# Activations of the gate spread over the down projection, PSUM in two pools, early weight halves moved from GpSimd to VectorE

## The chip, the core and the metric

The kernel runs on one core of one Trainium2 chip. The metric is the device time of one execution in microseconds; the time before is the median of three runs. The engines of the core are called PE (TensorE, the matrix multiplications; PEld is its loading of stationary operands), DVE (VectorE), ACT (ScalarE), POOL (GpSimd) and SP (SyncE, which here issues most of the transfers).

## The reference, cut to what matters

One layer over 1024 tokens of 1024 channels: a mixer, then a router, then sixteen experts, each of which takes the 128 tokens that score highest for it. All is float32.

```python
def expert_choice_ffn(h, w_r, w1, w3, w2):
    bn, n, _ = h.shape
    cap = EC_FACTOR * n // N_EXPERTS                      # 128
    aff = jax.nn.softmax((h @ w_r).astype(jnp.float32), axis=-1)
    gate, idx = lax.top_k(jnp.swapaxes(aff, 1, 2), cap)
    bidx = jnp.arange(bn)[:, None, None]
    xe = h[bidx, idx]
    hid = jax.nn.silu(jnp.einsum('becd,edf->becf', xe, w1)) * jnp.einsum('becd,edf->becf', xe, w3)
    ye = jnp.einsum('becf,efd->becd', hid, w2) * gate[..., None].astype(h.dtype)
    return jnp.zeros_like(h).at[bidx, idx].add(ye)

def reference(...):
    ...
        x = x + g1x * yx
        hx2 = rmsnorm(x, norm2_g[l]) * (1.0 + sc2x) + sh2x
        x = x + g2x * expert_choice_ffn(hx2, w_router[l], w1[l], w3[l], w2[l])
    return rmsnorm(x, final_g)
```

`w1` and `w3` are 1024x2048 for each expert, `w2` is 2048x1024.

## The kernel before, in words

**Products.** A float32 product is made of three matmuls: each operand is split into a rounded `hi` and the rest `lo`, and hi·hi, hi·lo and lo·hi are summed in PSUM. The weights of an expert come in 24 **units** of 128x2048 float32 (1 MB): eight each of w1, w3 and w2. A unit is loaded by SP into one of twelve buffers (`raw`), ACT copies it to `hi` (L104), and another engine subtracts, `lo = raw - hi` (L105). `presplit(n, engine)` does that for all units up to number n. `unit(key)`, called when PE comes to a unit, first splits ahead, up to two units past this one, always with DVE; the pool of the halves (`sp`) has three buffers, so a copy waits until PE has finished the unit three before.

**Experts.** The program is written in the order in which each engine shall work; nothing reorders it. One pass of the loop over e does: `up("3", e)` (eight units, matmuls L1251, L1253 and L1255 into four PSUM banks; in the first unit all three for two banks, then for the other two), with the gathered rows of the next expert transposed in between; `hidden(e)`, four multiplications on DVE, silu times the second product (L1270); `up("1", e+1)`, with the transposes of the hidden rows of e in between; `silu(e+1)`, four activations on ACT (L1264), one per bank; and `down(e)`, eight units (L1292, L1295, L1298) into two banks, then the evacuation (L1305) and a scatter-add by POOL. The pass e = 14 leaves out its `down`, so that `up("3", 15)` follows `silu(15)` directly; `down(14)` and `down(15)` come at the end.

**PSUM.** All results in PSUM come out of one pool of eight banks, taken in turn.

**Before the experts.** The router's scores of the last tile of tokens give, on DVE, sorted lists: MAX and MATCH_REPLACE steps, and compare steps L1017 and L1018, queued in `fills` and called one by one between other work by `fill(n)`. `router_sm(7)` is the softmax of the last tile (row sum L986 ... product `tv` L992). The end of the sort is the threshold T (L1176). From it come each token's place (`pos`, L1198), the one-hot matrix of an expert (`oh`, L1212, `route_oh`), its list of rows (`route`: `ix` L1223, `gate` L1224, the gather of rows `xe` by POOL L1229), and their transposes (L1239 to L1241), on which the first `up("1", 0)` waits. The halves of the first units are made along the way: unit 0, then 1, then 2, with POOL doing the subtraction; units 3 and 4, in a pool `sx` of their own, with DVE.

Of the kernel before, what the change touches and what calls it, by code (L numbers as in the profile page):

```python
# [20 lines left out]
P = 128  # L21
# [6 lines left out]
class Two:  # L28
    """a tensor in two tiles, halved along its second axis"""
# [16 lines left out]
def hybrid_layer(ctx, tc, x, c, ctxt, c_ctx, w_mod, b_mod, norm1_g, norm2_g, w_in, sgu_g, sgu_w,  # L46
# [13 lines left out]
    psp = ctx.enter_context(tc.tile_pool(name="ps", bufs=8, space=bass.MemoryType.PSUM))  # L60
# [6 lines left out]
    def bank(shape, name):  # L67
        return psp.tile(shape, F32, name=name, tag="bk")
# [8 lines left out]
    # ---- weights of the experts: loaded in units; each unit split into exact halves  # L77
# [41 lines left out]
    # ================================================================ phase 1  # L119
# [6 lines left out]
    # ---- loads of the first stage  # L126
# [10 lines left out]
    def wblk(n):  # L137
        """raw block n of 128 columns of w_in, loaded in pairs"""
        if n // 2 not in wraw:
            t = wb.tile([P, 8, 2 * P], F32, name="wraw")  # L140
            col = wcols[n // 2]
            nc.sync.dma_start(t, w_in[:, col:col + 2 * P].rearrange("(k p) f -> p k f", p=P))
            wraw[n // 2] = t
        return wraw[n // 2][:, :, (n % 2) * P:(n % 2 + 1) * P]
# [14 lines left out]
    # ---- constants  # L159
# [26 lines left out]
    # ---- parameter columns  # L186
# [6 lines left out]
    def rstd(dst, ssq, m, n, gap=lambda: None):  # L193
        """1 / sqrt(ssq / n + eps), refined by one Newton step; m is scratch"""
# [12 lines left out]
    # silu of the conditioning  # L207
# [12 lines left out]
    # ---- row normalisation: context in columns 8, 9 of stat  # L220
# [10 lines left out]
    def row_nr(o, n):  # L231
        """a Newton step for 1 / sqrt"""
# [9 lines left out]
    # 8 * log_sigmoid(lam), with log1p(z) = 2 atanh(z / (2 + z))  # L242
# [31 lines left out]
    # ---- modulation vectors: shift and scale of the first norm, as columns  # L274
# [54 lines left out]
    # ---- transposed, modulated inputs in exact halves  # L329
# [10 lines left out]
    def modsplit(srcs, k, s, hi, lo):  # L340
        """(src * scale + shift) of blocks k.. as hi + lo; a subtraction on DVE follows one step behind"""
# [17 lines left out]
    # ---- channel-major products with a block of 128 columns of w_in  # L359
# [8 lines left out]
    # ---- the other modulation vectors (gate 1, shift 2, scale 2, gate 2): rows summed on DVE, partitions on PE  # L368
# [37 lines left out]
    # ---- the first two blocks over all positions, transposes three steps ahead of the products  # L406
# [80 lines left out]
    # ---- recurrent branch: positions in the order (context, latent) forwards, (latent, context) backwards  # L487
# [110 lines left out]
    # ---- other channel-major blocks: u, then the gate of the recurrence  # L598
# [66 lines left out]
    # ---- gx (gelu, times the recurrence); meanwhile the remaining modulation vectors  # L665
# [7 lines left out]
    def split_wv(h, t):  # L673
        """(high, low) of the rows of block k"""
# [57 lines left out]
    # ---- v, token-major; gating of each chunk  # L732
# [65 lines left out]
    def scale_wo(h, ts):  # L798
        """gate 1 folded into the columns of w_out"""
# [62 lines left out]
    # ---- output projection, residual, second norm, router  # L862
# [24 lines left out]
    # scores by expert: one or two tiles in halves, each in 32 partitions  # L887
# [32 lines left out]
    def fill(n=1):  # L920
        """the next n steps of each queue; a number in the first queue waits for that many steps of the second"""
# [16 lines left out]
    # channels 256 q + 2 p + k of the second norm lie in the order (q k p)  # L938
# [64 lines left out]
    # ---- descending lists of the scores of each expert; the steps are queued and run between other work  # L1003
# [4 lines left out]
    def q_bitonic(n, v, dst, f=fills):  # L1008
        """v, n rows rising and then falling (or the reverse) -> descending"""
# [13 lines left out]
    def q_sort(i, dst, f=fills):  # L1023
        """the halves in WS[i] sorted and merged into dst, one row of CAP for each tile"""
# [14 lines left out]
    def q_fold(s, dst):  # L1039
        """rows 32.. joined to rows ..32: the CAP largest of each pair, descending"""  # L1040
# [64 lines left out]
    # the last tile, one half of the columns after the other  # L1105
# [32 lines left out]
    # by token and expert: the token, the score in exact halves, the token  # L1138
# [20 lines left out]
    presplit(1, G)  # L1159
# [8 lines left out]
    q_sort(5, L5)  # L1168
    while fills or fills2:
        fill()  # L1170
    presplit(2, G)
    # threshold: the 128th of the merged descending lists
# [4 lines left out]
    V.tensor_sub(tvr[:, :, :, 2], affs, tvr[:, :, :, 1])  # L1177
# [6 lines left out]
    # counts over the tiles before, four zero tiles in front  # L1184
# [14 lines left out]
    presplit(3, G)  # L1199
    pes.close()  # L1200

    # ================================================================ experts
# [13 lines left out]
    def route(e):  # L1216
        oh = OH.pop(e)
        p = bank([P, 4], "pr")
# [13 lines left out]
    def transpose_x(e):  # L1232
# [3 lines left out]
        for h in range(2):  # L1236
            p = bank([P, 4, P], "xp")
# [21 lines left out]

    def silu(e, pt):  # L1260
        sg[e] = []
        for b in range(4):
            s = mb.tile([P, 4, P], F32, name="sg", bufs=4)
            A.activation(s.rearrange("t j p -> t p j"), pt[b].rearrange("t (p j) -> t p j", j=4), AF.Silu)  # L1264
            sg[e].append(s)
# [6 lines left out]
    def transpose_h(e, bs):  # L1272
        for b in bs:
            p = bank([P, 4, P], "hp")
# [41 lines left out]
    while pieces:  # L1316
        load_next()
    presplit(4, V, sx)
    route_oh(1)
    presplit(5, V, sx)  # L1320
    g2row = mp.tile([P, D], F32, name="g2row")
# [7 lines left out]
    for e in range(NE):  # L1329
# [17 lines left out]
        if nxt:  # L1347
            hidden(e, up("3", e, mid))
            p1 = up("1", e + 1, {2: lambda: transpose_h(e, (0, 1)), 4: lambda: transpose_h(e, (2, 3))})
            silu(e + 1, p1)  # L1350
            if e + 2 < NE:
                down(e)
# [11 lines left out]
    # ================================================================ last expert's sum, final norm  # L1364
# [129 lines left out]
```

## Time and profile before

| | us |
|---|---|
| median of three runs | 1681.43 (1681.33 to 1681.81) |
| span of the profiled execution, first to last instruction | 1676.8 |
| of it PE / DVE / ACT / POOL busy | 1546.4 / 1394.0 / 1092.8 / 213.9 |

The span is 4.6 us less than the median, which holds what lies around the instructions too. The busy times are sums over the whole span: first the mixer and the router (to about 484 us), then the experts (to about 1660 us). The trace gives each instruction's start and length; several of one kind that follow closely stand in one row with their count (x4).

### The profile page before, as it was taken

The page shows a single profiled execution, that of the slowest core. Times are in us where ns is not written, and L with a number is a line of the kernel's source. Part 1 is how long each engine was busy: PE and PEld are TensorE (multiplying, and loading weights), DVE is VectorE, ACT ScalarE, POOL GpSimd, SP SyncE. Part 2 cuts the span into 40 slices and gives each one's busy share as a digit, 9 for nine tenths or more (in the row PEclk, how much of TensorE's full clock was granted, in tenths as well). Part 3 has the DMA queues.
Part 4 walks back from the last instruction along what each step waited for, and adds up shares of the span by engine and source line. Part 5 has one row for each costly group of instructions (what it writes and reads, how often), then busy time and mean ns, then how long its engine had stood idle before and what let it go on. Part 6 is the DMA issues. An engine that isn't in the chain of part 4 may idle for free.

```text
span 1676.8 us, 19242 instructions
## 1 busy us (share of the span) xinstructions
PE 1546.4 (92%) x7290; PEld 1262.6 (75%) x7290; DVE 1394.0 (83%) x1358; ACT 1092.8 (65%) x995; POOL 213.9 (13%) x160
## 2 busy tenths in 40 slices
PE   5899989889729999999999999999999999999995
PEld 2687779778627787877878787787877878788783
DVE  6669787867876898988989888898988989888897
ACT  6575746422326767777676777767777677777764
POOL 2411212532320000100101000010000101001002
PEclk8999999999859999999999999999999999999998
DMA  9010247333656999999999999999999999999855
GB/s 377 27 35 29 95 146 262 137 117 121 251 206 251 353 386 359 380 342 369 379 358 384 348 384 351 368 375 370 371 346 372 380 356 385 339 389 363 328 190 201
DMA packets 85932, 485.31 MB, mean 289 GB/s; under 512 B 11208, under 2 KB 20048, under 8 KB 35664
## 3 DMA queue, kind: packets, MB, share of 16 engines
q1 hardware_dynamic: 80912, 466.72, 72.8%
q0 software_dynamic: 4832, 17.33, 4.1%
q8 instruction: 57, 0.93, 0.2%
q14 instruction: 35, 0.29, 0.1%
q10 hardware_dynamic: 96, 0.03, 0.0%
HBM read 463.61 MB, written 20.45 MB: 289 GB/s over the span
## 4 chain that ended last, share of the span: by engine, by line
PE 68%; DVE 13%; ACT 10%; issue 4%; DMA 3%; POOL 2%; SPq 0%; ACTq 0%; DVEq 0%; POOLq 0%
PE h L1251 14%; PE h L1253 14%; PE h L1255 13%; PE ye L1295 6%; PE ye L1298 6%; PE ye L1292 5%; ACT sg L1264 3%; DVE lo L105 2%; ACT hi L104 2%; PE hp L1276 2%; DMA ring<-in_w_mod_dram 1%; PE pw L910 1%; PE pw L912 1%; PE xp L1239 1%; PE pw L914 1%
## 5 line engine op out<-in xcount | busy, mean ns | idle before, releaser
L105 DVE TENSOR_TENSOR lo<-raw,hi 128x2048 fp32r<-128x2048 f32 x381 | 863.3, 2290 | 154.1 <-ACT hi L104 152.8
L104 ACT ACTIVATE hi<-raw 128x2048 fp32r<-128x2048 f32 x384 | 733.3, 1919 | 260.7 <-PE h L1255 127.7
L1251 PE MATMUL h<-hi,xth 128*128 128x512 f32 x1024 | 288.6, 398 | 1.8 <-ACT hi L104 1.8
L1253 PE MATMUL h<-lo,xth 128*128 128x512 f32 x1024 | 282.2, 392 | 2.3 <-DVE lo L105 2.3
L1255 PE MATMUL h<-hi,xtl 128*128 128x512 f32 x1024 | 282.1, 392 | 0.0
L1253 PEld LDWEIGHTS h<-lo,xth 128*128 128x128 f32 x1024 | 192.6, 188 | 46.3 <-DVE lo L105 3.1
L1255 PEld LDWEIGHTS h<-hi,xtl 128*128 128x128 f32 x1024 | 192.5, 188 | 42.8
L1251 PEld LDWEIGHTS h<-hi,xth 128*128 128x128 f32 x1024 | 188.0, 189 | 40.4 <-ACT hi L104 2.7
L1295 PE MATMUL ye<-lo,hth 128*128 128x512 f32 x512 | 162.3, 398 | 18.5 <-DVE lo L105 18.5
L1292 PE MATMUL ye<-hi,hth 128*128 128x512 f32 x512 | 161.2, 396 | 0.0
L1298 PE MATMUL ye<-hi,htl 128*128 128x512 f32 x512 | 160.5, 394 | 0.0
L1308 POOL DMA_INDIRECT x2d<-ye,ix x15 | 50.1, 3340 | 815.4 <-DVE ye L1305 815.4
L1295 PEld LDWEIGHTS ye<-lo,hth 128*128 128x128 f32 x512 | 95.3, 188 | 46.2 <-DVE lo L105 24.6
L1298 PEld LDWEIGHTS ye<-hi,htl 128*128 128x128 f32 x512 | 96.3, 188 | 22.9
L1292 PEld LDWEIGHTS ye<-hi,hth 128*128 128x128 f32 x512 | 96.0, 188 | 22.3
L1264 ACT ACTIVATE sg<-h 128x512 f32<-128x512 f32 x64 | 62.9, 1146 | 2.2 <-PE h L1255 1.3
L1279 ACT ACTIVATE hth<-hp 128x512 fp32r<-128x512 f32 x64 | 35.0, 596 | 43.4 <-PE hp L1276 43.4
L388 DVE SCALAR_TENSOR_TENSOR ring<-ring,cs 128x1024 f32<-128x1024 f32 x28 | 46.0, 1642 | 11.9 <-DMA ring<-in_w_mod_dram 11.3
L362 PE MATMUL pu<-hxh,wh 128*128 128x512 f32 x128 | 50.9, 398 | 2.6 <-ACT g1row L721 2.6
L1229 POOL DMA_INDIRECT xe<-hx2d,ix x16 | 17.1, 1070 | 272.0 <-DVE gate L1224 241.2
L363 PE MATMUL pu<-hxh,wl 128*128 128x512 f32 x128 | 50.8, 397 | 0.0
L364 PE MATMUL pu<-hxl,wh 128*128 128x512 f32 x128 | 50.8, 397 | 0.0
(349 smaller groups left out, 1991.2 us busy)
## 6 DMA issues: line engine op xcount, KB each, us to landing
raw<-in_w_dram SPq DMA_DIRECT2D x383, 1024.0 KB, 7.3
ring<-in_w_mod_dram SPq DMA_DIRECT2D x32, 512.0 KB, 5.3
wmod<-in_w_mod_dram SPq DMA_DIRECT2D x8, 1024.0 KB, 9.6
wraw<-in_w_in_dram SPq DMA_DIRECT2D x6, 1024.0 KB, 7.1
xh<-in_x_dram SPq DMA_DIRECT2D x4, 1024.0 KB, 16.2
wor<-in_w_out_dram SPq DMA_DIRECT2D x4, 1024.0 KB, 8.4
xr<-in_x_dram SPq DMA_DIRECT2D x8, 512.0 KB, 4.3
x2d<-xr SPq DMA_DIRECT2D x8, 512.0 KB, 2.7
```

The source lines that it names most:

```text
L104: A.activation(hi, s, AF.Copy)
L105: eng.tensor_tensor(lo, s, hi, op=OP.subtract)
L362: PE.matmul(p, w[0][:, k], act[0][:, k], start=(k == 0), stop=False)
L363: PE.matmul(p, w[1][:, k], act[0][:, k], start=False, stop=False)
L364: PE.matmul(p, w[0][:, k], act[1][:, k], start=False, stop=(k == 7))
L1251: PE.matmul(pt[b], hi[:, k], wh[:, b * 512:(b + 1) * 512], start=(k == 0), stop=False)
L1253: PE.matmul(pt[b], hi[:, k], wl[:, b * 512:(b + 1) * 512], start=False, stop=False)
L1255: PE.matmul(pt[b], lo[:, k], wh[:, b * 512:(b + 1) * 512], start=False, stop=(k == 7))
L1264: A.activation(s.rearrange("t j p -> t p j"), pt[b].rearrange("t (p j) -> t p j", j=4), AF.Silu)
L1292: PE.matmul(pt[n], hi[:, j], wh[:, j2 * 1024 + n * 512:j2 * 1024 + n * 512 + 512], start=st_, stop=False)
L1295: PE.matmul(pt[n], hi[:, j], wl[:, j2 * 1024 + n * 512:j2 * 1024 + n * 512 + 512], start=False, stop=False)
L1298: PE.matmul(pt[n], lo[:, j], wh[:, j2 * 1024 + n * 512:j2 * 1024 + n * 512 + 512], start=False, stop=en)
```

## The change

Five things are different. The SILU of one bank gets a function of its own, and for e up to 13 the four are called after units 0, 2, 4 and 6 of `down(e)` instead of ahead of it. PSUM is one pool of eight banks until the experts begin; then it is a pool of six (h, ye, rb, fp) and one of two (pr, xp, hp), which wait tile by tile. The subtraction of unit 0 goes from POOL to DVE, at the same place of the program. Those of units 1 and 2 go from POOL to DVE, and from behind the sort and behind `pos` to behind `route(0)`; `route_oh(1)` is called ahead of units 3 and 4. A subtraction into `tvr` goes from behind T into the queue of sort steps. Comments are gone; lines after are higher by two or three.

```diff
@@ def hybrid_layer
-    psp = ctx.enter_context(tc.tile_pool(name="ps", bufs=8, space=bass.MemoryType.PSUM))
+    pss = ExitStack()
+    psp = pss.enter_context(tc.tile_pool(name="ps", bufs=8, space=bass.MemoryType.PSUM))
...
-    def bank(shape, name):
-        return psp.tile(shape, F32, name=name, tag="bk")
+    banks = [psp, psp]
+
+    def bank(shape, name, small=0):
+        return banks[small].tile(shape, F32, name=name, tag="bk")
@@ sort
-    presplit(1, G)
+    presplit(1, V)
     router_mm(7)
     fill(12)
     router_sm(7)
...
     q_sort(5, L5)
+    fills.insert(8, lambda: V.tensor_sub(tvr[:, :, :, 2], affs, tvr[:, :, :, 1]))
     while fills or fills2:
         fill()
-    presplit(2, G)
...
     V.tensor_reduce(T, m, axis=AX.X, op=OP.min)
-    V.tensor_sub(tvr[:, :, :, 2], affs, tvr[:, :, :, 1])
...
     V.scalar_tensor_tensor(pos, gt, FAR, eq, op0=OP.add, op1=OP.add)
-    presplit(3, G)
     pes.close()
@@ route, transpose_x, transpose_h
-        p = bank([P, 4], "pr")
+        p = bank([P, 4], "pr", 1)
...
-            p = bank([P, 4, P], "xp")
+            p = bank([P, 4, P], "xp", 1)
...
-            p = bank([P, 4, P], "hp")
+            p = bank([P, 4, P], "hp", 1)
@@ silu
+    def silu1(e, pt, b):
+        s = mb.tile([P, 4, P], F32, name="sg", bufs=4)
+        A.activation(s.rearrange("t j p -> t p j"), pt[b].rearrange("t (p j) -> t p j", j=4), AF.Silu)
+        sg.setdefault(e, []).append(s)
+
     def silu(e, pt):
-        sg[e] = []
         for b in range(4):
-            s = mb.tile([P, 4, P], F32, name="sg", bufs=4)
-            A.activation(s.rearrange("t j p -> t p j"), pt[b].rearrange("t (p j) -> t p j", j=4), AF.Silu)
-            sg[e].append(s)
+            silu1(e, pt, b)
@@ ahead of the experts, after route(0) and the loads
+    presplit(3, V)
+    route_oh(1)
     presplit(4, V, sx)
-    route_oh(1)
     presplit(5, V, sx)
+    pss.close()
+    for i, n in enumerate((6, 2)):
+        banks[i] = ctx.enter_context(tc.tile_pool(name=f"ps{n}", bufs=n, space=bass.MemoryType.PSUM,
+                                                  reuse_waits="tile"))
     g2row = mp.tile([P, D], F32, name="g2row")
@@ loop over e
             hidden(e, up("3", e, mid))
             p1 = up("1", e + 1, {2: lambda: transpose_h(e, (0, 1)), 4: lambda: transpose_h(e, (2, 3))})
-            silu(e + 1, p1)
             if e + 2 < NE:
-                down(e)
+                down(e, {u: lambda b=b: silu1(e + 1, p1, b) for b, u in enumerate((0, 2, 4, 6))})
+            else:
+                silu(e + 1, p1)
```

On ACT, from the middle of `up("1", 1)` to the transposes of the next expert in the middle of `up("3", 1)`, the program of before has these instructions in a row (`hth` are the transposed hidden rows, `sg` the SILU's output, `h_...` its bank):

```order
L1279 ACTIVATE hth<-hp 128x512 x2
L104 ACTIVATE hi<-raw 128x2048 x3
L1264 ACTIVATE sg<-h_4319 128x128x4
L1264 ACTIVATE sg<-h_4320 128x128x4
L1264 ACTIVATE sg<-h_4321 128x128x4
L1264 ACTIVATE sg<-h_4322 128x128x4
L104 ACTIVATE hi<-raw 128x2048 x11
L1240 ACTIVATE xth<-xp 128x512 x2
```

The changed program has at the same place:

```order
L1282 ACTIVATE hth<-hp 128x512 x2
L107 ACTIVATE hi<-raw 128x2048 x4
L1263 ACTIVATE sg<-h_4326 128x128x4
L107 ACTIVATE hi<-raw 128x2048 x2
L1263 ACTIVATE sg<-h_4327 128x128x4
L107 ACTIVATE hi<-raw 128x2048 x2
L1263 ACTIVATE sg<-h_4328 128x128x4
L107 ACTIVATE hi<-raw 128x2048 x2
L1263 ACTIVATE sg<-h_4329 128x128x4
L107 ACTIVATE hi<-raw 128x2048 x4
L1241 ACTIVATE xth<-xp 128x512 x2
```

The four activations stood together ahead of the copy for the third unit of `down`; now that copy stands ahead of the first of them, and two copies stand between any two.

On PE, at the first unit of a later `up("1", e+1)`, directly behind `up("3", e)`, the program of before has these matmuls, with the semaphores that each waits for (`h1_...` are the four banks, DVE_49 is the semaphore that DVE raises, at a value of each wait's own):

```order
L1251 MATMUL h1_5373<-hi_5322,xth_5256 128x512 [waits Activation_49]
L1251 MATMUL h1_5374<-hi_5322,xth_5256 128x512 [waits PE_49]
L1253 MATMUL h1_5373<-lo_5323,xth_5256 128x512 [waits DVE_49]
L1253 MATMUL h1_5374<-lo_5323,xth_5256 128x512
L1255 MATMUL h1_5373<-hi_5322,xtl_5257 128x512
L1255 MATMUL h1_5374<-hi_5322,xtl_5257 128x512
L1251 MATMUL h1_5375<-hi_5322,xth_5256 128x512 [waits PE_49]
L1251 MATMUL h1_5376<-hi_5322,xth_5256 128x512 [waits DVE_49,PE_49]
```

The changed program has:

```order
L1252 MATMUL h1_5380<-hi_5329,xth_5263 128x512 [waits Activation_49]
L1252 MATMUL h1_5381<-hi_5329,xth_5263 128x512
L1254 MATMUL h1_5380<-lo_5330,xth_5263 128x512 [waits DVE_49]
L1254 MATMUL h1_5381<-lo_5330,xth_5263 128x512
L1256 MATMUL h1_5380<-hi_5329,xtl_5264 128x512
L1256 MATMUL h1_5381<-hi_5329,xtl_5264 128x512
L1252 MATMUL h1_5382<-hi_5329,xth_5263 128x512 [waits DVE_49]
L1252 MATMUL h1_5383<-hi_5329,xth_5263 128x512 [waits DVE_49]
```

The third and fourth bank each have a wait for DVE of their own now. By the values of the semaphore and the addresses of the banks, they are the first two banks of `up("3", e)`, and the two waits are for the first and the second multiplication of `hidden(e)`; in the program of before no bank of `up("1", e+1)` was one of `up("3", e)`.

On DVE, at the end of the last tile's norm (`hx`), the program of before goes straight on with the steps of the sort:

```order
L1155 SCALAR_TENSOR_TENSOR hx_3494<-tm,ss_2519,SH2row 128x512 x2
L1017 TENSOR_TENSOR L_2542<-bt_3532 32x64
L1018 TENSOR_TENSOR L_2542<-bt_3532 32x64
L1049 TENSOR_TENSOR bt<-LS_2539,L_2542 32x128
L1028 MAX S_2522<-W_2520 64x8
```

The changed program has there:

```order
L1158 SCALAR_TENSOR_TENSOR hx_3494<-tm,ss_2519,SH2row 128x512 x2
L108 TENSOR_TENSOR lo<-raw,hi 128x2048
L1020 TENSOR_TENSOR L_2542<-bt_3532 32x64
L1021 TENSOR_TENSOR L_2542<-bt_3532 32x64
L1052 TENSOR_TENSOR bt<-LS_2539,L_2542 32x128
L1031 MAX S_2522<-W_2520 64x8
```

The subtraction of unit 0 stands ahead of the steps that `fill(12)` calls. The other two have joined the two that stood behind the first `gate` already, on both sides of `oh`:

```order
L1225 TENSOR_REDUCE gate<-pr 128x1
L108 TENSOR_TENSOR lo<-raw,hi 128x2048 x2
L1213 TENSOR_TENSOR oh<-iota_s,pos 128x1024
L108 TENSOR_TENSOR lo<-raw,hi 128x2048 x2
L1242 TENSOR_TENSOR xtl<-xp,xth 128x512 x2
```

So DVE does four of these subtractions, where it did two, between the first routing and the first transposes.

## Rows read from the trace of the kernel before

**Rows 1.** The page, part 4: the chain that ended last, by line.

```profile
PE h L1251 14%; PE h L1253 14%; PE h L1255 13%; PE ye L1295 6%; PE ye L1298 6%; PE ye L1292 5%; ACT sg L1264 3%; DVE lo L105 2%; ACT hi L104 2%; PE hp L1276 2%; DMA ring<-in_w_mod_dram 1%; PE pw L910 1%; PE pw L912 1%; PE xp L1239 1%; PE pw L914 1%
```

**Rows 2.** Windows: us; busy us per engine; granted clock; DMA share; GB/s.

```profile
643.40:1430.97 787.57, 773.00 (x3521) 632.07 (x3520) 689.88 (x430) 577.32 (x375) 47.86 (x22) 1.00 0.97 367
667.32:714.99 47.67, 47.67 (x226) 39.49 (x224) 44.57 (x32) 34.14 (x23) 4.35 (x2) 1.00 1.00 377
```

**Rows 3.** Timeline of the sort: start, length, engine, line, operation [idle before <-releaser].

```profile
448.19 0.22 DVE L992 TENSOR_SCALAR tv<-ex,ss 128x16 f32<-128x16 f32 x1
...
452.52 0.21 DVE L1017 TENSOR_TENSOR L<-bt 32x64 f32<-32x64 f32 x1
...
454.49 1.90 ACT L104 ACTIVATE hi<-raw 128x2048 fp32r<-128x2048 f32 x1
...
456.46 4.50 POOL L105 TENSOR_TENSOR lo<-raw,hi 128x2048 fp32r<-128x2048 f32 x1 [5.79 <-ACT hi L104]
...
457.43 0.17 DVE L986 TENSOR_REDUCE ss<-pl 128x1 f32<-128x16 f32 x1 [0.25 <-PE pl L982]
...
458.24 2.75 DVE L992 TENSOR_SCALAR tv<-ex,ss 128x16 f32<-128x16 f32 x1
...
464.68 9.01 POOL L105 TENSOR_TENSOR lo<-raw,hi 128x2048 fp32r<-128x2048 f32 x2 [3.72 <-ACT hi L104]
...
464.80 4.52 DVE L1018 TENSOR_TENSOR bt<-bt 32x64 f32<-32x64 f32 x1
...
469.44 4.33 DVE L1017 TENSOR_TENSOR bt<-bt 32x64 f32<-32x64 f32 x1
...
480.73 0.27 DVE L1176 TENSOR_REDUCE T<-bt 32x1 f32<-32x128 f32 x1
```

**Rows 4.** Timeline of DVE after the first routing.

```profile
487.81 2.28 DVE L105 TENSOR_TENSOR lo<-raw,hi 128x2048 fp32r<-128x2048 f32 x1
...
498.07 0.69 DVE L1241 TENSOR_TENSOR xtl<-xp,xth 128x512 fp32r<-128x512 f32 x1 [4.64 <-ACT xth L1240]
```

**Rows 5.** Waits: engine, line, releaser: us in total, times, longest us.

```profile
PE ye L1295 <- DVE lo L105: 18.5, 14, 1.3
```

**Rows 6.** Timeline of the down projection of expert 1.

```profile
642.91 3.93 ACT L1264 ACTIVATE sg<-h 128x512 f32<-128x512 f32 x4
...
646.63 5.51 ACT L104 ACTIVATE hi<-raw 128x2048 fp32r<-128x2048 f32 x3
...
648.59 6.70 DVE L105 TENSOR_TENSOR lo<-raw,hi 128x2048 fp32r<-128x2048 f32 x3 [3.48 <-ACT hi L104]
...
648.98 0.63 PE L1292 MATMUL ye<-hi,hth 128*128 128x512 f32 x2
...
650.94 0.30 PEld L1295 LDWEIGHTS ye<-lo,hth 128*128 128x128 f32 x2 [1.76 <-DVE lo L105]
...
653.37 0.64 PE L1292 MATMUL ye<-hi,hth 128*128 128x512 f32 x2
...
656.16 0.63 PE L1292 MATMUL ye<-hi,hth 128*128 128x512 f32 x2
...
656.36 1.92 ACT L104 ACTIVATE hi<-raw 128x2048 fp32r<-128x2048 f32 x1 [0.87 <-PE ye L1298]
...
658.31 2.29 DVE L105 TENSOR_TENSOR lo<-raw,hi 128x2048 fp32r<-128x2048 f32 x1 [0.50 <-ACT hi L104]
```

**Rows 7.** Timeline of the end of up("3", 1) and the start of up("1", 2).

```profile
620.52 2.47 DVE L1270 TENSOR_TENSOR sg<-sg,h 128x512 f32<-128x512 f32 x4
...
620.98 0.41 PEld L1251 LDWEIGHTS h<-hi,xth 128*128 128x128 f32 x2
```

**Rows 8.** The multiplications of L1270: lengths in ns, least, median, most.

```profile
L1270 DVE TENSOR_TENSOR sg<-sg,h x64: 673/678/681, 548.5 to 1602.4; 128x512 f32<-128x512 f32 x64
```

**Rows 9.** Timeline of the start of up("1", 15).

```profile
1550.27 0.42 PEld L1251 LDWEIGHTS h<-hi,xth 128*128 128x128 f32 x2
...
1550.74 2.47 DVE L1270 TENSOR_TENSOR sg<-sg,h 128x512 f32<-128x512 f32 x4
```

## The prediction

> **What bounds the kernel now.** I read the chain that ended last first. After the mixer it runs almost wholly through the experts' matmuls: L1251 to L1255 and L1292 to L1298 hold 58% of the span [rows 1]. Eleven experts, from the start of `down(1)` to that of `down(12)`, take 787.57 us, 71.60 each, with PE busy 98% of it at the full granted clock, 1.00 [rows 2]. So in the experts only what stops PE counts: 14.6 us of 787.57 are left, and the next view accounts for nearly all of them. The view of waits names the largest stop: 18.5 us in 14 pieces, in which the second step of a unit of `down` waits for `lo` from DVE [rows 5].
>
> The timeline of one `down` tells which unit and why [rows 6]. Four activations hold ACT from 642.91 to 646.84; only then come the copies that `down` needs next. The copy for the third unit ends at 648.55, its subtraction (2.29) at 650.88, and PE goes on at 650.94, 0.06 later. The third unit starts at 648.98, the fourth at 653.37, 4.39 apart; an undisturbed unit takes 656.16 − 653.37 = 2.79. So PE loses 1.60 per `down`. It is a wait of one place, and the rest of `down` is at PE's pace.
>
> Ahead of the experts the bound is DVE's sort. There I looked for operations that are longer than their kind: `tv` takes 2.75 where another tile's took 0.22, and two compare steps take 4.52 and 4.33 where the usual is 0.21 [rows 3]. Each lies under a subtraction of POOL, and ends with it: `tv` at 460.99 (POOL: 460.96), the two compares at 469.32 and 473.77, with POOL's two in one stretch of 9.01 from 464.68 to 473.69. DVE's compares stand still while POOL subtracts.
>
> **The change part by part.** The sum is made against the profiled span, 1676.8, and carried over to the median, 1681.43, with the 4.6 us around the span unchanged.
>
> *1. Subtractions off POOL during the sort.* Gone: 2.75 − 0.22, 4.52 − 0.21 and 4.33 − 0.21, together 10.96 us of DVE's chain to T at 480.73 [rows 3].
>
> *2. The subtraction of unit 0 on DVE.* It stands ahead of the steps of `fill(12)`, which began at 452.52. It waits for ACT's copy, which ends at 454.49 + 1.90 = 456.39, then takes 2.29 [rows 3, 6]: it ends near 458.7. Queued behind it are the sort steps that filled 452.52 to 457.18 (L986 starts at 457.43 after 0.25 idle): 4.66 us, now to 463.4, and L986, the softmax and the last list's sort behind them. L986 is 463.4 − 457.4 = 6.0 later. The moved `tvr` step costs about one step more, 0.3 at most. T comes at 480.73 − 10.96 + 6.0 + 0.3, 4.7 earlier. Bounds: 11.0 earlier if DVE's wait were free; nothing if the compares run slow for a reason other than POOL.
>
> *3. The subtractions of units 1 and 2 behind `gate`.* DVE has 2 × 2.28 = 4.6 us more between 487.81 and the first `xtl` at 498.07, and was idle 4.64 there, waiting for the transposes that follow the gather [rows 4]. The gather and the wait shift together with T. I price it at 0; without that cover it is 4.6.
>
> *4. SILUs in `down`.* The copy for unit u+2 now starts when unit u does, 0.20 after (656.16 to 656.36), and its subtraction ends at 658.31 + 2.29 = 660.60, 4.44 after the unit's start [rows 6]. It is wanted in the second step of unit u+2, at 2 × 2.79 + 0.46 = 6.04 (0.46 is two of a unit's twelve matmuls in 2.79): 1.6 us to spare. A SILU, (3.93/4 = 0.98 in the row of four, a little more by itself) comes behind a copy that ends 2.12 after the unit's start, so it ends near 3.2, when the next copy is due at 2.99. The delay of 0.2 is inside the 1.6. ACT has 8 × 1.92 + 4 × 1.1 = 19.8 us of work in 8 × 2.79 = 22.3. So the 1.60 goes whole: 14 experts (e = 0 to 13), 22.4 us. Nothing new is late: `up("3", e+1)` takes over the SILUs' banks, and the last SILU, called after unit 6, is done near 6 × 2.79 + 3.2 = 19.9, before the 22.3 at which it begins.
>
> *5. Six banks instead of eight.* The third and fourth bank of `up("1", e+1)` now wait for the first and second multiplication of `hidden(e)`. In the row of four multiplications of 2.47 us, each takes 0.68 [rows 7, 8], so they start 0.60 apart: the second ends at 620.52 + 0.60 + 0.68 = 621.80, and PE knows it at 621.86. The weight load for the fourth bank stood at 620.98 + 0.23 = 621.21 [rows 7], so it is held for 0.65. Not all of a hold is lost: in rows 6 loads were idle 1.76 and the unit lost 1.60, 0.16 less. That makes 0.49, and 14 × 0.49 = 6.9 us for e = 0 to 13. For e = 14 the multiplications start later against PE: the second ends at 1552.02, seen at 1552.08, and the load stood at 1550.27 + 0.23 = 1550.50 [rows 9], so 1.58 − 0.16 = 1.4. Together 8.3. Such a wait is not in the trace of before. Bounds: 0, if the banks come free in time after all; and 32.0, if the third bank waited for all four (620.52 + 2.47 + 0.06 = 623.05 against a load at 620.98, 2.07 each, and 1550.74 + 2.47 + 0.06 − 1550.27 = 3.0 for e = 14, none of it recovered). I take 8.3: the order shows a wait of its own for each bank. The pool of two I price at 0: its pairs of transposes lie two units apart, over 5 us, and an evacuation takes 0.69 on DVE [rows 4]; if PE waited for one per expert, it would be 16 × 0.69 = 11.
>
> **Sum.** −4.7 − 22.4 + 8.3 = −18.8: span 1658.0, median 1681.43 − 18.8 = **1662.6 us**.
>
> **The rivals.**
>
> *The bank wait costs nothing.* If the multiplications start a little earlier against PE or the hold is absorbed, −27.1: 1654.3. For it: the hold is only 0.65 long. Against it: PE is busy 98%, with no slack behind.
>
> *The front gives nothing.* DVE's early wait for the copy, or `xtl` coming late behind four subtractions (4.6 of 4.64 idle is a narrow cover), eats the 4.7: −14.1, 1667.3.
>
> *Memory takes over.* At 367 GB/s an expert moves 26.3 MB; if that were the limit, the period would stay 71.60 and only the front's 4.7 come: 1676.7. Against it: a stretch of 47.67 us moved 377 GB/s [rows 2], at which 26.3 MB take 69.7 us, under the forecast period of 71.60 − 1.60 + 0.49 = 70.5. The Trainium skill, "HBM Reference", Specifications, gives an effective 358 GB/s per core, and about 425 for a core that streams alone. By the 358, 26.3 MB would take 73.4 us, an estimate from that page; this trace's 367 is above it, and the core is alone.
>
> *The other side: the stall only moves.* If the copies come late behind the SILUs, four small stalls take the place of one: no gain in `down`, and the banks' 8.3 stays: −4.7 + 8.3 = +3.6, 1685.0. It decides when a SILU holds the next subtraction for 1.6 + 0.4 = 2.0 us, so that four stalls of 0.4 give back the 1.60. Against it: a SILU takes 1 us and falls mostly into ACT's idle time.
>
> *The other side: banks wait as a whole.* With the 32.0 of part 5, −27.1 + 32.0 = +4.9: 1686.3. It decides from 27.1 / 15 = 1.8 us per expert. For it only that one semaphore serves many waits; against it the two separate waits.
>
> **How the numbers follow.** Of a measurement of this kernel, 0.2% (3.4 us) is about what can be told from no change. Chances: the forecast 0.66 (its own range 1658 to 1666: the hold between 0.2 and 0.65 per expert, the front between 2 and 8), free banks 0.12, no front 0.12, memory 0.03, moved stall 0.04, whole banks 0.03. Memory at 1676.7 is still faster by 0.28%. So faster 0.66 + 0.12 + 0.12 + 0.03 = 0.93 less some for what I don't see, 0.92; the last two lie just over 0.2% slower, and I split their 0.07 and the rest as slower 0.04, same 0.04. The range takes in free banks at its lower end and the front's loss at its upper: 1654 to 1668.
>
> **What would show it right or wrong.** Right: no wait of L1295's successor for `lo` left, the third and fourth unit of `down` 2.79 apart, a new wait of PE at the first unit of `up("1")` for the multiplications, near 0.5 each in 14 places and 1.4 in one, no compare step on DVE over 1 us in the sort, the first `xtl` near 493.4, and 70.5 us per expert. Wrong: waits for `lo` spread over `down`, copies of ACT waiting for loads in most units, or compares that are slow without POOL. What would upset the sum most is a wait of PE in the experts that I counted as covered, since it comes 14 times.

## The result and the profile after

The changed kernel takes 1660.67 us (median of four runs, 1656.74 to 1663.98) against 1681.62 for the kernel before (1681.33 to 1682.18): a ratio of 0.988, with a 95% interval of 0.987 to 0.990. In a second set of runs the ratio was 0.9875 (0.985 to 0.990). The profiled execution has a span of 1658.4 us where 1658.0 was forecast; its own time is 1660.27.

In the rows of the changed kernel the copy and the subtraction are L107 and L108, the matmuls of `up` L1252, L1254 and L1256, those of `down` L1295, L1298 and L1301, the SILU L1263 and the multiplication L1273: not every line is higher by two or three than before.

The experts first. A window from the start of `down(1)` to that of `down(12)`, eleven experts (us; busy us by engine with counts; granted clock; DMA share; GB/s):

```profile
638.06:1413.80 775.74, 774.66 (x3522) 632.38 (x3521) 693.04 (x430) 577.29 (x374) 47.90 (x22) 1.00 0.98 373
```

That is 70.52 us per expert, where [rows 2] had 71.60, and PE is idle for 1.1 us of it all instead of 14.6 (most of the new hold, below, lies inside the modelled length of a matmul and does not show as idle time of PE). The view of waits has no row any more in which `down` waits for `lo`, which [rows 5] had 14 times; it has a new one, for weight loads of the first unit of `up("1")` behind the multiplications, and a small one for weight loads of `up("3")` behind SILUs (engine, line, releaser: us in total, times, longest):

```profile
PEld h L1252 <- DVE sg L1273: 11.9, 30, 1.2
PEld h L1252 <- ACT sg L1263: 2.7, 4, 0.8
```

The four of the second row lie in `up("3", 0)` and `up("3", 15)`, which follow their four SILUs directly and take over their banks. The prediction has no such wait, but it costs nothing: the kernel before waited at the same two places for the copies behind the SILUs, and the two ups took 26.11 and 25.11 us there and take 26.03 and 25.07 here.

```profile
PEld h L1251 <- ACT hi L104: 2.7, 2, 1.5
```

The first row counts thirty loads in fifteen places: the third and the fourth bank each wait. The timeline of one of the places:

```profile
613.72 0.42 PEld L1252 LDWEIGHTS h<-hi,xth 128*128 128x128 f32 x2
...
614.63 2.47 DVE L1273 TENSOR_TENSOR sg<-sg,h 128x512 f32<-128x512 f32 x4
...
615.36 0.19 PEld L1252 LDWEIGHTS h<-hi,xth 128*128 128x128 f32 x1 [0.31 <-DVE sg L1273]
615.36 1.10 PE L1252 MATMUL h<-hi,xth 128*128 128x512 f32 x2
615.96 0.19 PEld L1252 LDWEIGHTS h<-hi,xth 128*128 128x128 f32 x1 [0.41 <-DVE sg L1273]
```

The loads of the third and fourth bank go out at 615.36 and 615.96, 0.60 apart as the multiplications are; without a wait they would follow at about 615.09 and 615.31 (six matmuls after 613.72). The hold of the second is 0.65, as forecast; what it costs shows in the length of a pair of ups, on average 48.21 us where it was 47.66, so 0.55.

In `down(1)` the copies, SILUs and subtractions interleave, and the third unit (643.64) is followed by the fourth 2.79 later (646.43), where [rows 6] had 4.39:

```profile
640.08 1.10 ACT L1263 ACTIVATE sg<-h 128x512 f32<-128x512 f32 x1
...
641.05 1.92 ACT L107 ACTIVATE hi<-raw 128x2048 fp32r<-128x2048 f32 x1
...
643.00 2.29 DVE L108 TENSOR_TENSOR lo<-raw,hi 128x2048 fp32r<-128x2048 f32 x1 [0.50 <-ACT hi L107]
...
643.64 0.62 PE L1295 MATMUL ye<-hi,hth 128*128 128x512 f32 x2
...
646.43 0.62 PE L1295 MATMUL ye<-hi,hth 128*128 128x512 f32 x2
```

A copy starts 0.20 after its unit, as before; the SILU lies ahead of it in ACT's idle time. A `down` takes 22.31 us, before 23.93.

The sort, against [rows 3]: the subtraction of unit 0 waits 3.82 for ACT's copy, the row sum L989 starts at 463.12, `tv` takes 0.23, no compare step is long, and T comes at 475.86.

```profile
454.40 1.90 ACT L107 ACTIVATE hi<-raw 128x2048 fp32r<-128x2048 f32 x1
...
456.33 2.29 DVE L108 TENSOR_TENSOR lo<-raw,hi 128x2048 fp32r<-128x2048 f32 x1 [3.82 <-ACT hi L107]
...
463.12 0.15 DVE L989 TENSOR_REDUCE ss<-pl 128x1 f32<-128x16 f32 x1
...
463.91 0.23 DVE L995 TENSOR_SCALAR tv<-ex,ss 128x16 f32<-128x16 f32 x1
...
475.86 0.27 DVE L1179 TENSOR_REDUCE T<-bt 32x1 f32<-32x128 f32 x1
```

Behind `gate`, four subtractions stand where two stood [rows 4], and the first transposes' `xtl` is not held: its idle time, 4.64 before, is 0.35.

```profile
482.94 4.48 DVE L108 TENSOR_TENSOR lo<-raw,hi 128x2048 fp32r<-128x2048 f32 x2
...
488.47 4.49 DVE L108 TENSOR_TENSOR lo<-raw,hi 128x2048 fp32r<-128x2048 f32 x2
...
493.31 0.69 DVE L1242 TENSOR_TENSOR xtl<-xp,xth 128x512 fp32r<-128x512 f32 x1 [0.35 <-ACT xth L1241]
```

### The profile page after: what moved, and what is told of

Read it like the earlier page. It is cut to its first block, busy times and chain, and to the rows that moved or that the text cites. A ratio compares the mean times of both kernels' runs of the same rounds, so it can differ in the third digit from the quotient of the medians.

```text
span 1658.4 us, 19225 instructions
## 1 busy us (share of the span) xinstructions
PE 1555.1 (94%) x7290; PEld 1266.5 (76%) x7290; DVE 1391.0 (84%) x1361; ACT 1093.0 (66%) x995; POOL 201.1 (12%) x157
## 4 chain that ended last, share of the span: by engine, by line
PE 65%; DVE 15%; ACT 8%; DMA 6%; issue 4%; POOL 2%; SPq 0%; DVEq 0%; POOLq 0%; ACTq 0%
PE h L1254 11%; PE h L1256 11%; PE h L1252 11%; PE ye L1295 7%; PE ye L1298 7%; PE ye L1301 7%; DVE lo L108 3%; DMA raw<-in_w_dram 3%; ACT hi L107 3%; PE hp L1279 2%; DMA ring<-in_w_mod_dram 1%; DVE sg L1273 1%; DMA ctx_sb<-in_ctx_dram 1%; PE xp L1240 1%; POOL wor L806 1%
## 5 line engine op out<-in xcount | busy, mean ns | idle before, releaser
L108 DVE TENSOR_TENSOR lo<-raw,hi 128x2048 fp32r<-128x2048 f32 x384 | 874.2, 2291 | 140.1 <-ACT hi L107 138.9
L107 ACT ACTIVATE hi<-raw 128x2048 fp32r<-128x2048 f32 x384 | 736.5, 1920 | 241.3 <-PE h L1256 159.5
L1252 PE MATMUL h<-hi,xth 128*128 128x512 f32 x1024 | 294.9, 402 | 3.5 <-ACT sg L1263 1.2
L1254 PE MATMUL h<-lo,xth 128*128 128x512 f32 x1024 | 282.7, 393 | 2.0 <-DVE lo L108 2.0
L1256 PE MATMUL h<-hi,xtl 128*128 128x512 f32 x1024 | 282.0, 392 | 0.0
L1252 PEld LDWEIGHTS h<-hi,xth 128*128 128x128 f32 x1024 | 188.1, 189 | 51.7 <-DVE sg L1273 11.9
L1254 PEld LDWEIGHTS h<-lo,xth 128*128 128x128 f32 x1024 | 192.7, 188 | 45.1 <-DVE lo L108 2.8
L1256 PEld LDWEIGHTS h<-hi,xtl 128*128 128x128 f32 x1024 | 192.5, 188 | 42.9
L1295 PE MATMUL ye<-hi,hth 128*128 128x512 f32 x512 | 161.1, 396 | 0.0
L1301 PE MATMUL ye<-hi,htl 128*128 128x512 f32 x512 | 160.5, 394 | 0.0
L1298 PE MATMUL ye<-lo,hth 128*128 128x512 f32 x512 | 160.5, 394 | 0.0
L1298 PEld LDWEIGHTS ye<-lo,hth 128*128 128x128 f32 x512 | 96.4, 188 | 22.7
L1301 PEld LDWEIGHTS ye<-hi,htl 128*128 128x128 f32 x512 | 96.4, 188 | 22.6
L1295 PEld LDWEIGHTS ye<-hi,hth 128*128 128x128 f32 x512 | 96.2, 189 | 22.2
L1263 ACT ACTIVATE sg<-h 128x512 f32<-128x512 f32 x64 | 69.6, 1107 | 0.2 <-PE h L1256 0.2
```

Source lines behind the costliest of these rows:

```text
L107: A.activation(hi, s, AF.Copy)
L108: eng.tensor_tensor(lo, s, hi, op=OP.subtract)
L1252: PE.matmul(pt[b], hi[:, k], wh[:, b * 512:(b + 1) * 512], start=(k == 0), stop=False)
L1254: PE.matmul(pt[b], hi[:, k], wl[:, b * 512:(b + 1) * 512], start=False, stop=False)
L1256: PE.matmul(pt[b], lo[:, k], wh[:, b * 512:(b + 1) * 512], start=False, stop=(k == 7))
L1295: PE.matmul(pt[n], hi[:, j], wh[:, j2 * 1024 + n * 512:j2 * 1024 + n * 512 + 512], start=st_, stop=False)
```

## The experiments

The theory was that the change is three things that add: VectorE's sort steps freed of GpSimd (−4.7), the SILUs out of the way of the third unit of `down` (−22.4), and banks of the pool of six that come free late (+8.3). The rivals: that the gain comes from the split of PSUM, that the split costs nothing, and that the front gives nothing. Times between executions of one kernel differ by several us here, so beside the medians I read three stretches inside each profile: from the start of the norm's second half (`hx`) to T, the mean of the pairs `up("3", e)`, `up("1", e+1)` that lie between two downs, and the mean of the fourteen downs.

| kernel | median us (runs) | ratio to before of the same set, 95% | `hx` to T | pair of ups | down |
|---|---|---|---|---|---|
| before | 1681.62 (4) | | 28.87 | 47.66 | 23.93 |
| changed | 1660.67 (4) | 0.988 (0.987 to 0.990) | 24.09 | 48.21 | 22.31 |
| front alone | 1675.48 (8) | 0.997 (0.996 to 0.998) | 24.08 | 47.66 | 23.92 |
| changed, front undone | 1664.15 (5) | 0.991 (0.990 to 0.993) | 28.88 | 48.21 | 22.31 |
| changed, SILUs together | 1683.43 (8) | 1.002 (1.001 to 1.003) | 24.08 | 48.20 | 23.92 |
| changed, first units reordered | 1652.81 (5) | 0.984 (0.982 to 0.985) | 24.08 | 47.66 | 22.31 |
| changed, again | 1659.89 (4) | 0.988 (0.985 to 0.990) | 24.03 | 48.21 | 22.31 |
| changed, no split | 1654.41 (5) | 0.984 (0.981 to 0.986) | 24.04 | 47.66 | 22.31 |
| changed, unit 0 late | 1657.16 (4) | 0.986 (0.983 to 0.988) | 20.82 | 48.20 | 22.31 |
| no split, unit 0 late | 1648.97 (5) | 0.982 (0.979 to 0.984) | 20.83 | 47.66 | 22.31 |
| the same, copy early | 1647.37 (4) | 0.979 (0.978 to 0.981) | 19.38 | 47.66 | 22.31 |
| the same, in a gap | 1647.94 (4) | 0.980 (0.979 to 0.982) | 18.31 | 47.66 | 22.31 |
| changed, unit 0 on GpSimd | 1656.63 (4) | 0.986 (0.984 to 0.988) | 20.85 | 48.21 | 22.31 |

The kernel before, run beside them in three sets, had medians of 1680.25 (16 runs), 1680.56 (9) and 1680.81 (7).

### Front alone

```diff
-    presplit(1, G)
+    presplit(1, V)
...
-    presplit(2, G)
...
-    presplit(3, G)
...
+    presplit(3, V)
+    route_oh(1)
     presplit(4, V, sx)
-    route_oh(1)
     presplit(5, V, sx)
```

> The kernel before with the moved subtractions alone (units 0 to 2 on VectorE, the step into tvr in the sort's queue); SILUs and PSUM as before. Main theory: GpSimd's subtractions held VectorE's compare steps, 10.96 us go and about 6 come back with the wait for ACT's copy, so T comes near 476.0, the first matmul of the experts near 493.4, the rest as before: about 4.7 us faster than before, near 1676.9, with the waits of the down projection for lo (14 of 1.3) unchanged. Rival, the gain is given back behind gate (four subtractions ahead of xtl): T early but the first matmul where it was, 1681.6. Rival, VectorE does not stand still because of GpSimd: compare steps of over 4 us remain, 1681.6 or later.

Measured: 4.8 us less than before by the medians, and 4.79 less from the norm to T. The waits of `down` are the old ones:

```profile
PE ye L1293 <- DVE lo L105: 18.6, 14, 1.3
```

So the front gives its gain alone and whole.

### Front undone

The reverse edit, on the changed kernel.

> The changed kernel with the subtractions of units 0 to 2 back on GpSimd at their old places; SILUs in the down projection and PSUM split as changed. Main theory: the parts add, so this is 4.7 us slower than the changed kernel, near 1665.4, with 22.3 us per down projection and 48.2 per up pair as in the changed kernel, and compare steps of over 4 us in the sort again. Rival, the parts lean on each other: another time than the sum, by more than 3 us.

Measured: 1664.15, 0.991 of before where the changed kernel has 0.988, so some 5 us slower; 4.79 of it lies between the norm and T. GpSimd's subtractions and the long steps are back in the sort, and end together again (463.23 + 9.02 = 472.25 and 468.00 + 4.33 = 472.33):

```profile
463.23 9.02 POOL L108 TENSOR_TENSOR lo<-raw,hi 128x2048 fp32r<-128x2048 f32 x2 [3.72 <-ACT hi L107]
...
463.36 4.52 DVE L1021 TENSOR_TENSOR bt<-bt 32x64 f32<-32x64 f32 x1
...
468.00 4.33 DVE L1020 TENSOR_TENSOR bt<-bt 32x64 f32<-32x64 f32 x1
```

The parts add.

### SILUs together

```diff
-            if e + 2 < NE:
-                down(e, {u: lambda b=b: silu1(e + 1, p1, b) for b, u in enumerate((0, 2, 4, 6))})
-            else:
-                silu(e + 1, p1)
+            silu(e + 1, p1)
+            if e + 2 < NE:
+                down(e)
```

> The changed kernel with the four SILUs ahead of the down projection again; PSUM split and the front as changed. Main theory: the 22.6 us of the down projections come back (third unit 1.6 late, 14 waits for lo of 1.3), the waits for banks stay (about 9 us in 14 places), so about 1683.3, slower than before by some 4 us of the split less the front's 4.8. Rival, the gain came from the split of PSUM and not from the place of the SILUs: near 1661. Rival, the waits for banks come only with the SILUs in the down projection: near 1676.8.

Measured: 1683.43, slower than before. Both waits are in it, the old one of `down` and the new one of the first up unit:

```profile
PE ye L1298 <- DVE lo L108: 18.6, 14, 1.3
PEld h L1252 <- DVE sg L1273: 12.0, 30, 1.2
```

The gain belongs to the SILUs' place, and the split alone is a loss that the front's gain does not cover.

### First units reordered

Unit 1 is begun for the first two banks before unit 0 is done for the other two.

```diff
+            if two and k == 0:
+                w0 = unit((which, e, 0))
+                mms(0, w0, (0, 1))
+                mms(1, ready[nused[0]], (0, 1))
+                mms(0, w0, (2, 3))
+            elif two and k == 1:
+                mms(1, unit((which, e, 1)), (2, 3))
```

> The changed kernel, in which the first two units of the up projection with w1 (from expert 1 on) are done for the first two banks, then for the other two, so that the third bank is wanted 1.4 us later. Main theory: the hold of 0.65 us per expert (0.54 of it lost, 14 times, and 1.4 at expert 15) goes, nothing else waits: 9 us faster than the changed kernel, near 1651.7, up pairs at 47.66 instead of 48.2. Rival, the copy of unit 3, which waits for unit 0's later end, makes up for it: a new wait for hi or lo at unit 3 of up to 1 us per expert, near 1660. Rival, the 0.55 that an up pair grew was not the banks but something else: near 1660 without waits for sg.

Measured: 1652.81, 6 to 8 us under the changed kernel by the ratios, where 9 were expected; inside the profile, from the start of the first up matmul to that of the last, 1078.22 us against 1087.08, 8.9 less. The row of waits for `sg` is gone, and PE is never idle in eleven experts:

```profile
639.30:1408.90 769.60, 769.60 (x3521) 633.21 (x3520) 690.75 (x430) 576.03 (x374) 47.91 (x22) 1.00 0.99 376
```

The banks were the whole of the 0.55 per pair. Loads keep up at 376 GB/s.

### The changed kernel again

No edit.

> The changed kernel as it is, beside the next three on the same chip, for their differences and for its own spread. Main theory: 21 us faster than the kernel before. The parts of its spans that differ between executions lie in the mixer, ahead of the sort; 22.3 us per down projection and 48.2 per up pair are the same in each.

Measured: 1659.89 in a set where the kernel before took 1680.56. Its profiled execution (1661.8) is 3.4 longer than the first one (1658.4). Up pairs, downs and the sort agree to 0.1; the norm's second half starts 2.7 later (454.50 against 451.77), and the first pair of ups, with `up("1", 0)`, takes 0.7 more (74.96 against 74.25). So most of the difference lies ahead of anything that the change touched.

### No split

The SILUs in `down` and the moved subtractions, in the kernel before with its one pool of eight:

```diff
     psp = ctx.enter_context(tc.tile_pool(name="ps", bufs=8, space=bass.MemoryType.PSUM))
...
-            silu(e + 1, p1)
             if e + 2 < NE:
-                down(e)
+                down(e, {u: lambda b=b: silu1(e + 1, p1, b) for b, u in enumerate((0, 2, 4, 6))})
+            else:
+                silu(e + 1, p1)
```

> The moved subtractions and the four SILUs in the down projection, but one pool of eight banks as before. Main theory: the split is the whole cause of the waits of the first up unit for the multiplications, and not needed for the SILUs: the banks that the down projection takes here were transposes of hidden rows, and the next up takes two of them and two of the SILUs' banks, read long before. So 9 us faster than the changed kernel, near the kernel with the reordered first units (27.4 faster than before), up pairs at 47.66. Rival, the SILUs hold banks longer and the ring of eight runs short: a new wait of up(3) or of the transposes for SILUs, 1 us or more per expert, 1660 to 1667.

Measured: 1654.41, 5.5 under the changed kernel of the same set, less than the 9 that were expected. The mechanism is as expected: pairs of ups at 47.66, no wait for `sg` and none for SILUs, 69.98 us per expert.

```profile
639.20:1409.00 769.80, 769.80 (x3523) 633.40 (x3522) 692.18 (x430) 577.79 (x375) 47.89 (x22) 1.00 0.99 376
```

In the profiled execution the rest went elsewhere: the first pair of ups took 76.07 and the last 74.13, where the run with reordered units had 73.97 and 72.65; the granted clock, 1.00 in those stretches of the changed kernel's profile, was 0.97 from 520 to 575 and 0.96 from 1530 to 1575 here. Seen finer (windows with the columns as above), it was 0.50, the lower of its two levels (1.2 GHz instead of 2.4), in two stretches:

```profile
529.20:532.60 3.40, 3.40 (x11) 2.69 (x10) 3.40 (x2) 0.66 (x1) 0.00 (x0) 0.50 0.90 289
1560.00:1563.40 3.40, 3.14 (x7) 2.48 (x8) 3.40 (x3) 1.48 (x1) 0.00 (x0) 0.50 0.65 193
```

Half of these 6.8 us, 3.4, is an estimate of their cost, and about what is missing. Ahead of the first fall PE had stood idle twice, in `up("3", 0)`, for the copy and the subtraction behind the four SILUs:

```profile
526.31 1.20 PE L1249 MATMUL h<-hi,xth 128*128 128x512 f32 x4 [0.76 <-ACT hi L104]
...
528.64 1.64 PE L1251 MATMUL h<-lo,xth 128*128 128x512 f32 x4 [1.13 <-DVE lo L105]
```

Around the second it was `up("3", 15)`, with 1.07 and 1.12. All six profiles with the one pool of eight have the two idle times; three of them show a fall in the first pair and two in the last. In the seven with the split, PE's idle times in `up("3", 0)` are three and shorter (0.34, 0.38 and 0.82), and none shows a fall in either pair. So the split seems to spare the kernel some of this; no run tests it by itself.

The run with both changes below, on the same pool, has 72.73 in the last pair. The split is not needed for the SILUs.

### Unit 0 late

```diff
-    presplit(1, V)
     router_mm(7)
     fill(12)
     router_sm(7)
+    presplit(1, V)
```

> The changed kernel with the subtraction of unit 0 on VectorE behind the softmax of the last tile instead of ahead of the sort steps. Main theory: the wait for ACT's copy and the 2.29 no longer stand ahead of 4.7 us of steps; the subtraction lies where VectorE waits 1.0 for the last scores. T comes 6.0 - 1.3 = 4.7 earlier, near 471.2 against a start of the last norm near 451.8, and so does everything behind: 4.7 us faster than the changed kernel. Rival, the transfer or ACT's copy of a later unit sets the start of the experts: less than 1.5 us.

Measured: 1657.16, 2.7 under the changed kernel of the same set; 3.2 from the norm to T, where 4.7 were expected. `presplit` issues ACT's copy too, and the copy had moved along, to behind the softmax's exponential:

```profile
459.06 1.90 ACT L107 ACTIVATE hi<-raw 128x2048 fp32r<-128x2048 f32 x1
...
459.40 0.23 DVE L995 TENSOR_SCALAR tv<-ex,ss 128x16 f32<-128x16 f32 x1
460.99 2.29 DVE L108 TENSOR_TENSOR lo<-raw,hi 128x2048 fp32r<-128x2048 f32 x1 [1.36 <-ACT hi L107]
```

VectorE waits 1.36 for it. My expectation had forgotten one of the moved step's two instructions.

### Both

No split, and unit 0 late.

> One pool of eight banks, SILUs in the down projection, subtractions off GpSimd, that of unit 0 behind the softmax: the last two together. Main theory: the gains add, 9.0 + 4.7 = 13.7 us faster than the changed kernel, near 1647, the fastest of all. Rival: with the start of the experts earlier, loads come late (ACT's copies wait for them), and less than 9 is left.

Measured: 1648.97, 10.9 under the changed kernel of the same set, where 13.7 were expected: inside the profile 3.2 of the front, for the reason found in unit 0 late, and 8.2 of the experts (1079.77 from the first to the last up matmul, against 1087.92). What the experts lack lies in the first pair of ups, 75.44: the granted clock was 0.50 in 5.1 us of it, against 2.9 us in the changed kernel of the same set. ACT's copies wait for loads 22.8 us in all, less than in the kernel before (35.2), and a pair of ups stays at 47.66.

### Copy early

ACT's copy of unit 0 where it was, VectorE's subtraction behind the softmax.

```diff
-    presplit(1, V)
+    hi0 = sp.tile([P, 2048], F32R, name="hi")
+    lo0 = sp.tile([P, 2048], F32R, name="lo")
+    A.activation(hi0, units[0][1], AF.Copy)
     router_mm(7)
     fill(12)
     router_sm(7)
+    V.tensor_tensor(lo0, units[0][1], hi0, op=OP.subtract)
+    ready[0] = (hi0, lo0)
+    nsplit[0] = 1
```

> Eight banks in one pool, SILUs in the down projection, and the subtraction of unit 0 behind the softmax, but ACT's copy left at its early place (in the two runs before it had moved along, and VectorE waited 1.36 for it). Theory: from the last half of the norm to T 24.05 - 6.0 + 1.3 = 19.4 us, where it was 20.83 with the late copy: 1.4 us faster than that. Rival, the subtraction cannot begin earlier for another reason: 20.8 again.

Measured: 19.38 from the norm to T where 19.4 was expected, and 1647.37, the fastest of all medians (0.979 of before).

### In a gap

The same subtraction between `route_oh(0)` and `route(0)`.

> As the run before, but the subtraction of unit 0 still later, between the one-hot matrix of expert 0 and its list, where VectorE waits 2.19 us for the matmuls of the list. Theory: from the norm to T 24.05 - 6.0 = 18.1 us, and from T to the first matmul of the experts 17.4 + 0.1 as before: 1.2 us faster than the run before. Rival, the first matmul or the loads behind unit 0's buffer come late: from T to the first matmul over 18.5.

Measured: 18.31 to T, and 17.68 from T to the first matmul of the experts, where the run before had 17.41. Together 0.8 earlier, where 1.2 were expected, as the subtraction now fills the gap and a little more (it starts at 476.93, and `ix`, which waits for nothing now, at 479.20); the medians, 1647.94 and 1647.37, don't tell the two apart.

```profile
475.79 1.22 DVE L1212 TENSOR_TENSOR oh<-iota_s,pos 128x1024 fp32r<-128x1024 f32 x1
476.93 2.28 DVE L1316 TENSOR_TENSOR lo<-raw,hi 128x2048 fp32r<-128x2048 f32 x1
479.20 0.16 DVE L1223 CAST ix<-pr 128x1 int32<-128x1 f32 x1
```

### Unit 0 on GpSimd

```diff
-    presplit(1, V)
+    presplit(1, G)
```

> The changed kernel with the subtraction of unit 0 alone back on GpSimd, units 1 and 2 on VectorE behind gate. It prices the two sides of that one step. Theory: VectorE's wait and work of 6.0 us go and the 2.53 us that the softmax stood still come back: from the norm to T 24.05 - 6.0 + 2.5 = 20.6, so moving unit 0 was a loss of 3.5 us inside the gain of 4.8. Rival, the three subtractions on GpSimd count alike: about 4.8 x 2 / 3 of the gain left, 25.7.

Measured: 20.85 from the norm to T, 3.2 less than in the changed kernel, and 1656.63. `tv` stands still again until GpSimd ends (453.32 + 4.49 = 457.81, and 455.09 + 2.75 = 457.84):

```profile
453.32 4.49 POOL L108 TENSOR_TENSOR lo<-raw,hi 128x2048 fp32r<-128x2048 f32 x1 [5.79 <-ACT hi L107]
...
455.09 2.75 DVE L995 TENSOR_SCALAR tv<-ex,ss 128x16 f32<-128x16 f32 x1
```

Of the front's three moves, then, two gained 8 us and the move of unit 0 gave 3.2 of it back: it took away 2.5 us of standing still and put 5.8 of waiting and work in its place (24.09 against the 18.31 of the run in a gap, which has nothing of unit 0 ahead of T on VectorE).

## Why the prediction was right

**The base.** The forecast of the span, 1658.0, met 1658.4; that of the median, 1662.6, met 1660.67. The weak step is the one that put 4.6 us around the span. In every execution whose span is on record, of the kernel before too, the time is 1.7 to 2.0 above the span; so the profiled execution of the kernel before was about 2.7 faster than the median that I set it beside. That the two spans agree within 0.4 is in part luck: in both profiles the norm's second half starts at the same time (451.86 and 451.77), while over all profiles it starts from 448.72 to 454.50. The stretches inside the profiles don't depend on that.

**Parts 1 and 2, the sort.** Forecast 4.7 earlier; T came 4.87 earlier (480.73 to 475.86), 4.78 from the norm. The run with the front alone and the run with the front undone show it from both sides, and the run in a gap, which has neither ahead of T, shows the size of the two terms: the release of VectorE 28.87 − 18.31 = 10.6 (forecast 10.96 less 0.3 for the moved step), the wait for the copy and the subtraction 24.09 − 18.31 = 5.8 (forecast 6.0). The mechanism is one that the Trainium skill states, "SBUF — State Buffer", Who interferes with whom: a VectorE instruction with two SBUF inputs and a GpSimd instruction that reads SBUF exclude each other, and the one issued second waits for all of the first. The trace agrees in both kernels that have it: the compare steps, 0.2 us long, took 4.52 and 4.33, to the end of the subtraction that had begun. `tv`, which has one tensor and a column as its inputs, stood still as well (2.75); no run here tells why.

**Part 3, behind `gate`.** Priced at 0, and it cost 0, with 0.35 of the 4.64 us left: from T to the first matmul of the experts it is 17.36 us before, 17.32 with the front alone and 17.48 in the changed kernel.

**Part 4, the SILUs.** Forecast 14 × 1.60 = 22.4; a down went from 23.93 to 22.31, 14 × 1.62 = 22.6. The stall did not move elsewhere: all downs are at 22.30 to 22.32.

**Part 5, the banks.** Forecast 14 × 0.49 + 1.4 = 8.3. The fourteen places took 7.6 (0.44 in the first pair, 0.55 in the others), and the last pair of ups 1.42 (72.65 to 74.07): 9.0. The hold was 0.65 as worked out; a little less of it came back than I had taken from the other stall. The reordered units and the kernel without the split each take the wait away, and the pair is back at 47.66. The pool of two, priced at 0, cost nothing: no row of the view has a transpose that waits for an evacuation.

The 0.44 of the first pair can't be read by itself. That pair takes 73.81 to 76.07 in the thirteen profiles, of which 1.3 to 6.2 us had a granted clock of 0.50. With half of that time taken off, an estimate, it is 73.5 to 73.6 in the six profiles with the wait for banks and 72.9 to 73.1 in the seven without: 0.5 to 0.6, as in the other pairs.

**Sum.** In the profiles −4.8 − 22.6 + 9.0 = −18.4, and the span fell by 18.4.

**Rivals.** Free banks and a front without gain are out by the profile, memory by 376 GB/s at 69.96 us per expert (first units reordered), the moved stall by the downs; that banks wait as a whole is out by the two waits 0.60 apart.

Left open: what makes the mixer's length differ between executions of one kernel. Its start goes with the granted clock. Where that is 0.91 over the first 60 us (two profiles), one and the same step of the mixer (a modulation, L353, or L350 in the kernels made from the one before) starts at 52.9 to 53.1; at 0.86 (five) it starts at 54.0 to 56.0, and at 0.83 (six) at 56.8 to 57.6. The rest, up to the norm, isn't explained by it: the two profiles of the changed kernel have 59.6 and 58.2 us at 0.50 ahead of the norm, and reach it 2.7 apart.

## What to carry to other kernels

When activations stand in a row ahead of the copies that feed the matrix engine, place them one by one where their engine idles; what a place holds is the slack of the queue behind it, here 1.6 us against a SILU of 1.1. Before splitting a PSUM pool, ask which result inherits which bank and how late that bank's last reader is: eight banks in one ring cost nothing here, and six cost 0.55 us in each expert and 1.42 at the last. Before moving a subtraction from GpSimd to the engine that it holds up, count what it waits for: up to the first matmul of the experts, the same subtraction cost 5.8 us ahead of the sort, 1.1 behind the softmax with its copy early, and about 0.3 in a gap.

## What the runs showed that was not expected

The split of PSUM, which came with the SILUs in one edit, wasn't needed for them and was the only part that cost time in the experts; what it may spare, two stretches at half the clock in the run without it, showed only beside that run. The move of unit 0, part of the front's gain by its look in the diff, was a loss of 3.2 us. And one kernel's executions spread over 7 to 8 us (the changed kernel 1656.74 to 1663.98; the kernel before 1676.11 to 1684.26 in one set), though the stretches of the experts between the first and the last agree within 0.1 us per pair: in the profiles, the second half of the last tile's norm starts anywhere from 448.72 to 454.50, in code that is the same. Differences below some 4 us were told apart only by stretches inside the profiles.
